# The first two k-tiles of a trunk kernel: scale and shift by TensorE in column groups instead of VectorE dots

## The chip, the cores and the metric

The kernel runs on one core of a Trainium2 chip. The metric is the device time of one execution in microseconds (us), lower is better; a run's time is that of its program on the one core. Before the change the median of three runs is 1251.24 us (1250.53 to 1252.52).

## What is computed

The reference is a two-layer decoder trunk on 256 tokens of width 2048, batch 1. Layer 0 is a Mamba-2 mixer, layer 1 a dilated sliding-window attention over keys and values made from layer 0's output. Only the very beginning of layer 0 matters here:

```python
def _adaln(c, w, b):
    mod = jax.nn.silu(c) @ w + b
    shift, scale, gate = jnp.split(mod, 3, axis=-1)
...
for layer in range(DEPTH):
    shift, scale, gate = _adaln(c, ada_w[layer], ada_b[layer])
    h = x * (1.0 + scale) + shift
    y = _ssd_mixer(h, a_in_w[i], ...)      # proj = h @ in_w; z, xBC, dt = split(proj)
```

`c` is one vector of 2048 numbers, `ada_w` a matrix of 2048 x 6144 for each layer, and `in_w` of layer 0 is 2048 x 10304. So nothing of `h @ in_w` can be computed before a scale and a shift for some of h's 2048 columns have been made out of silu(c) and ada_w.

## The kernel before, in words

**Tiles.** The contraction of 2048 is cut into 16 k-tiles of 128 (kt = 0 to 15). h is kept transposed, 128 rows of a k-tile by 256 tokens, as two tiles: `hhi`, a rounded copy, and `hlo`, what the rounding left (both are named actT in the profile). Weights come as pieces of 512 KB (`raw`, 128 x 1024); each piece is split into `whi` (a copy by ScalarE, L99) and `wlo` (the difference, by VectorE, L101), and TensorE adds three products, hi x hi, hi x lo and lo x hi, into PSUM. There are six buffers of raw and four each of whi and wlo. A piece of the kind "b", "x" or "h" is 24 matmuls of 256 columns (L144 to L146), a piece of the kind "z" 12 of 512 (L198 to L200).

**Scale and shift.** silu(c) stands in all 128 partitions (`cb_`, 1 MB, a broadcast load, L63, and a SiLU by ScalarE, L68). A "column" of ada_w (`araw`, 1 MB, L272) holds, in each partition, the 2048 weights of one output; VectorE multiplies it by cb_ and sums along the row (the dot, L279). Two columns, scale and shift, make a k-tile's modulation; the bias `adab` is added (L284), ScalarE makes h (L444) and its rounded copy (L445), VectorE the remainder (L446). `h_step` does one column; two buffers in each of two pools hold four columns.

**The order of the work.** The begin stage runs through a list of 58 pieces, written out by hand in eight rows, such as "b4:0. b6:0. h z2:0. b2:0 x1:0 h". "z6:2" is piece 2 (k-tiles 4 and 5) of the output block z6; "h" is one of the 16 pieces of the first two blocks, which are accumulated through the whole stage. The list is made so that each piece needs only the k-tiles whose scale and shift exist by then: partial sums of a block are put away in SBUF (`put_away`, L519) and taken up again later. In each step of the loop a piece is fetched (five to six ahead), the next one is split, the piece's matmuls are issued, and about four columns are dotted for seven pieces (`h_step`). All loads of the stage are issued by SyncE's queue, in the order of the program, each waiting for its buffer and for the load eight places before it. After the stage follow the blocks' remaining products, the state-space scan, the output projection and layer 1; none of that is touched.

Of the kernel before, what the change touches and what calls it, by code (L numbers as in the profile page):

```python
# [18 lines left out]
P = 128  # L19
L = 256  # L20
# [29 lines left out]
def trunk(ctx, tc, xT, x, c, par, cst, bias, lnrow, ada, wdt, win, wxs, wout, wk, wv, wbin, wbout, out):  # L50
# [16 lines left out]
    bcast(cb_, c)  # L67
    S.activation(cb_, cb_, AF.Silu)  # L68
# [4 lines left out]

    cons.tile([P, 32], F32, name="pad")
# [243 lines left out]
    with ExitStack() as cA:  # L318
# [14 lines left out]
        with ExitStack() as cS:  # L333
# [4 lines left out]
            begun = {("z", 0): (win[6], 6, szt[0]), ("z", 1): (win[7], 4, szt[1]),  # L338
                     ("xs", 1): (win[5], 4, as_cm(y[0])), ("bc", 2): (win[1], 4, as_cm(y[1])),
                     ("z", 2): (win[8], 14, y[2]), ("bc", 4): (win[2], 12, as_cm(y[3])), ("z", 4): (win[10], 6, y[4]),  # L340
                     ("bc", 6): (win[3], 12, as_cm(y[5])), ("z", 6): (win[12], 10, y[6]), ("z", 5): (win[11], 8, y[7])}
# [39 lines left out]
            def product(kind, g, pre=None):  # L381
# [5 lines left out]
                if src is None:  # L387
                    src = win[{"bc": g // 2, "xs": 4 + g, "z": 6 + g}[kind]]
# [23 lines left out]
            with ExitStack() as c0:  # L412
# [4 lines left out]
                raws, xts, late = [], {}, []  # L417
# [10 lines left out]
                def h_step():  # L428
# [4 lines left out]
                    if kind == "scale" and kt % 2 == 0 and kt:  # L433
                        fetch_x(kt)
                    ada_dot(0, kind, kt, raw)
                    if kt > 1:
                        pin[0] = None
# [11 lines left out]
                h_step.i = 0  # L449
# [5 lines left out]
                for row in ("b4:0. b6:0. h z2:0. b2:0 x1:0 h", "b2:1. x1:1. z1:0 z1:1. z4:0 h h",  # L455
# [3 lines left out]
                    for w in row.split():  # L459
                        if w == two:  # L460
                            n = -2 if sum(o[0] == -2 for o in order) == sum(o[0] == -1 for o in order) else -1
                            order.append((n, sum(o[0] == n for o in order), False))
                        else:
                            order.append((w[:2], int(w[3]), w[-1] == "."))
                order[-5:-5] = [("dt", 0, False), ("dt", 1, False)]
                source = {"dt": wdt, -2: win[0], -1: win[4], **{n: p[0] for n, p in zip(names, begun.values())}}
                pss = {-2: first[0], -1: first[1]}
# [6 lines left out]

                fetch()
                fetch()
                fetch_x(0)
                nc.sync.dma_start(adab_, par[:, :NB])
                V.tensor_scalar(adab[:, :, :, 1:3], adab[:, :, :, 1:3], 1.0, None, op0=ALU.add)
# [3 lines left out]
                fetch_piece()  # L483
                for _ in range(2):
                    for _ in range(2):
                        h_step()
                    while late:
                        pin[0] = late.pop()().ins
                    fetch_piece()
# [31 lines left out]
                begin, done, ended, halves = {}, set(), [], {}  # L521
                for i, (k, q, ends) in enumerate(order):
                    fetch_piece()
                    if i == 16:
                        nc.sync.dma_start(prm, par[:, NB:])
# [10 lines left out]
                    z = str(k)[0] == "z"  # L536
# [4 lines left out]
                    if z:  # L541
# [8 lines left out]
                    while h_step.i < min(len(cols), 4 + (i + 1) * 4 // 7):  # L550
# [118 lines left out]
            def firsts(kind, g):  # L669
# [3 lines left out]
                if src is None:  # L673
                    src = win[{"bc": g // 2, "xs": 4 + g, "z": 6 + g}[kind]]
# [443 lines left out]
def _layout(x, c, ada_w, ada_b, ln_g, ln_b, a_in_w, a_conv_w, a_conv_b, a_dt_bias,  # L1118
# [29 lines left out]
    def mask(delta, win_, dil):  # L1148
# [6 lines left out]
    ada = ada_w.reshape(2, D, 3, KT, P).transpose(0, 2, 3, 4, 1)  # L1155
# [4 lines left out]
    win = _pieces(np.concatenate([bc, xs[:, :1024], z], 1))  # L1160
    return {
        "xT": x[0].T.reshape(KT, P, L).transpose(1, 0, 2), "x": x[0], "c": c, "par": par, "cst": cst, "bias": bias,
# [25 lines left out]
```

## Time and profile before

| what | value |
|---|---|
| median of three runs | 1251.24 us |
| the profiled execution's own time | 1249.66 us |
| its span on the core | 1247.9 us |
| TensorE (PE) busy | 1216.1 us, 97% |
| VectorE (DVE) busy | 1030.6 us, 83% |
| ScalarE (ACT) busy | 703.4 us, 56% |
| moved by DMA | 335.88 MB, 269 GB/s on the mean |
| granted TensorE clock | 0.999 of full |

The profile is of one execution. A row of the timeline has the start in us from the span's start, the duration, the engine, the source line, the operation, the tile written and the tile read, the shapes and a count, and in brackets how long the engine had been idle and what released it. PEld is TensorE's weight load, SPq are the loads as SyncE issues them. A row of stretches has, for each engine, its busy time and in brackets the number of instructions; then the granted clock (PEclk), the mean busy share of the 16 DMA engines, and GB/s. A row of waits has the engine and line that waited, the one it waited for, the sum in us, how often, and the longest.

### The profile page before, as it was taken

How to read it: one execution, taken by the hardware profiler on the slowest of the kernel's cores; microseconds unless marked ns; L12 is line 12 of the kernel's file. 1: busy time of each engine (PE TensorE's matmuls, PEld its weight loads, DVE VectorE, ACT ScalarE, POOL GpSimd, SP SyncE). 2: the span in 40 equal slices, each digit the busy share in tenths (PEclk: the TensorE clock that was granted, in tenths of full speed). 3: DMA queues.
4: the chain of work that ended last, by engine and by line, in shares of the span. 5: the costliest groups of instructions: out<-in, count | busy, mean ns of one | idle time of the engine just before them, and what ended most of it. 6: DMA issues, size and time to landing. Idle time of an engine off the chain costs nothing.

```text
span 1247.9 us, 18743 instructions
## 1 busy us (share of the span) xinstructions
PE 1216.1 (97%) x7086; PEld 1041.6 (83%) x7086; DVE 1030.6 (83%) x1454; ACT 703.4 (56%) x1045; POOL 0.2 (0%) x4
## 2 busy tenths in 40 slices
PE   4999999999999999999999999999999999999997
PEld 4889998898888888778888788888888888888886
DVE  6999986999987989899768678879888867658777
ACT  3655477869588789654344544434445645445631
POOL 0000000000000000000000000000000000000000
PEclk9999999999999999999999999999999999999999
DMA  9999977687556456689988469989998774363641
GB/s 384 423 421 421 421 258 257 223 281 272 203 184 220 164 174 203 224 327 332 360 318 301 179 203 372 372 321 348 357 380 317 240 243 136 135 201 121 235 171 67
DMA packets 80586, 335.88 MB, mean 269 GB/s; under 512 B 9104, under 2 KB 9328, under 8 KB 67696
## 3 DMA queue, kind: packets, MB, share of 16 engines
q1 hardware_dynamic: 80496, 334.69, 73.5%
q8 instruction: 55, 0.90, 0.3%
q14 instruction: 35, 0.29, 0.1%
HBM read 332.47 MB, written 2.18 MB: 268 GB/s over the span
## 4 chain that ended last, share of the span: by engine, by line
PE 85%; DVE 7%; DMA 3%; ACT 2%; issue 2%; SPq 0%; DVEq 0%; ACTq 0%
PE acc L173 21%; PE acc L199 12%; PE acc L200 12%; PE acc L198 12%; PE acc L176 11%; PE acc L144 3%; PE acc L146 3%; PE acc L145 3%; DVE araw L279 2%; DVE wlo L101 2%; PE py L656 1%; DMA araw<-in_ada 1%; ACT whi L99 1%; DMA raw<-in_wv 1%; PE acc L851 1%
## 5 line engine op out<-in xcount | busy, mean ns | idle before, releaser
L99 ACT ACTIVATE whi<-raw 128x1024 fp32r<-128x1024 f32 x392 | 411.7, 1059 | 377.3 <-PE acc L200 144.1
L101 DVE TENSOR_TENSOR wlo<-raw,whi 128x1024 fp32r<-128x1024 f32 x392 | 473.8, 1222 | 137.0 <-ACT whi L99 132.6
L173 PE MATMUL acc<-actT,whi 128*128 128x512 f32 x1280 | 405.3, 397 | 0.0
L176 PEld LDWEIGHTS acc<-actT,wlo 128*128 128x128 f32 x1280 | 239.1, 188 | 59.1 <-DVE wlo L101 4.3
L199 PE MATMUL acc<-wlo,actT 128*128 128x512 f32 x688 | 269.8, 392 | 0.6 <-DVE wlo L101 0.5
L198 PE MATMUL acc<-whi,actT 128*128 128x512 f32 x688 | 266.5, 394 | 1.2 <-ACT actT L723 1.2
L176 PE MATMUL acc<-actT,wlo 128*128 128x256 f32 x1280 | 253.4, 279 | 1.7 <-DVE wlo L101 1.4
L279 DVE SCALAR_TENSOR_TENSOR araw<-araw,cb__72 128x2048 f32<-128x2048 f32 x96 | 219.4, 2286 | 12.0 <-DMA araw<-in_ada 11.9
L173 PEld LDWEIGHTS acc<-actT,whi 128*128 128x128 f32 x1280 | 195.9, 189 | 0.4
L200 PE MATMUL acc<-whi,actT 128*128 128x512 f32 x432 | 169.0, 391 | 0.0
L199 PEld LDWEIGHTS acc<-wlo,actT 128*128 128x128 f32 x688 | 129.3, 188 | 28.8 <-DVE wlo L101 2.8
L198 PEld LDWEIGHTS acc<-whi,actT 128*128 128x128 f32 x688 | 128.8, 188 | 27.0 <-ACT actT L723 1.7
L144 PE MATMUL acc<-actT,whi 128*128 128x256 f32 x384 | 108.9, 287 | 17.4 <-ACT actT L445 17.2
L145 PE MATMUL acc<-actT,whi 128*128 128x256 f32 x384 | 108.7, 285 | 0.0
L146 PE MATMUL acc<-actT,wlo 128*128 128x256 f32 x384 | 106.7, 285 | 1.9 <-DVE wlo L101 1.9
L200 PE MATMUL acc<-whi,ylo 128*128 128x512 f32 x256 | 100.7, 394 | 0.0
L200 PEld LDWEIGHTS acc<-whi,actT 128*128 128x128 f32 x432 | 81.1, 188 | 16.6
L144 PEld LDWEIGHTS acc<-actT,whi 128*128 128x128 f32 x384 | 74.1, 194 | 18.8 <-ACT actT L445 17.4
L146 PEld LDWEIGHTS acc<-actT,wlo 128*128 128x128 f32 x384 | 73.3, 194 | 2.2 <-DVE wlo L101 2.1
L145 PEld LDWEIGHTS acc<-actT,whi 128*128 128x128 f32 x384 | 74.5, 194 | 0.3
L200 PEld LDWEIGHTS acc<-whi,ylo 128*128 128x128 f32 x256 | 48.1, 188 | 9.7
L614 ACT ACTIVATE seg<-cbc,cumT 128x128 f32<-128x128 f32 x128 | 41.0, 390 | 4.9 <-DVE wlo L101 2.3
(262 smaller groups left out, 1054.6 us busy)
## 6 DMA issues: line engine op xcount, KB each, us to landing
araw<-in_ada SPq DMA_DIRECT2D x96, 1024.0 KB, 7.5
raw<-in_win SPq DMA_DIRECT2D x112, 512.0 KB, 6.7
raw<-in_wout SPq DMA_DIRECT2D x64, 512.0 KB, 5.4
raw<-in_wbin SPq DMA_DIRECT2D x64, 512.0 KB, 4.0
raw<-in_wxs SPq DMA_DIRECT2D x48, 512.0 KB, 4.4
raw<-in_wv SPq DMA_DIRECT2D x48, 512.0 KB, 6.3
raw<-in_wk SPq DMA_DIRECT2D x48, 512.0 KB, 7.5
cbc<-cumd SPq DMA_DIRECT2D x16, 512.0 KB, 5.0
```

The source lines that it names most:

```text
L99: copied.append(S.activation(hi, raw, AF.Copy))
L101: latest.append(V.tensor_tensor(lo, raw, hi.bitcast(F32), op=ALU.subtract))
L144: T.matmul(o, hi[:, k, c_], ahi[:, kt, :], start=first, stop=False, skip_group_check=True)
L145: T.matmul(o, hi[:, k, c_], alo[:, kt, :], start=False, stop=False, skip_group_check=True)
L146: T.matmul(o, lo[:, k, c_], ahi[:, kt, :], start=False, stop=kt == k1 - 1, skip_group_check=True)
L173: T.matmul(ps[n], hi[:, k, n * P:n * P + P], both(kt), start=kt == 0, stop=False, skip_group_check=True)
L176: T.matmul(ps[n][:, 0, :], lo[:, k, n * P:n * P + P], high(kt), start=False, stop=kt == KT - 1, skip_group_check=True)
L198: T.matmul(o, h_, hi[:, k, :], start=kt == k0, stop=False, skip_group_check=part)
L199: T.matmul(o, h_, lo[:, k, :], start=False, stop=False, skip_group_check=part)
L200: end = T.matmul(o, l_, hi[:, k, :], start=False, stop=kt == k1 - 1, skip_group_check=part)
L279: V.scalar_tensor_tensor(raw, raw, 1.0, cb_, op0=ALU.mult, op1=ALU.mult, accum_out=mod[layer][:, ct, j:j + 1])
L614: S.activation(seg[:, hh, b, :], cbc[:, hh, b, :], AF.Relu, bias=cumT[:, b, h0 + hh:h0 + hh + 1], scale=-1.0)
```

## The change

- **K-tiles 0 and 1 by TensorE.** Their columns of ada_w are laid out by rows instead (contraction in the partitions): four loads of 512 KB for each k-tile, each 128 x 1024, that hold four groups of 256 outputs (128 of shift, 128 of scale). c comes a second time as a small column tile (128 x 16, `ccol`); ScalarE's SiLU writes it into `ctile`, one column of every 32, the others zero. `ada_partial` runs four matmuls for each load, one for each group of 32 output partitions ("column group"), 256 columns wide, in fp32. `ada_sum` copies the 128 x 256 result (ScalarE), sums over the partitions by two matmuls against a column of ones, adds the bias (VectorE) and makes hhi (ScalarE) and hlo (VectorE, two instructions). The other 28 columns of layer 0's scale and shift stay dots.
- **Filler matmuls.** `keep_warm` runs 128 x 128 matmuls of ones into a PSUM tile that nobody reads: 10 at the start, 12 around k-tile 0's sums.
- **Buffers.** K-tile 0's four loads and k-tile 1's last lie in raw buffers, k-tile 1's first three in wlo buffers.
- **Loads.** The column of c and the bias adab are issued by ScalarE's queue; all others by SyncE's. The broadcast of c comes in two halves, behind the first four pieces, and its SiLU in two halves.
- **The "h" pieces.** The first two blocks (512 columns each, two k-tiles in a piece) become one of 1024 columns with one k-tile in a piece (`whead`, `head_piece`); still 16 pieces of 24 matmuls. The list begins with two of them: "h h b4:0. b6:0. z2:0. b2:0 x1:0", then "h b2:1. x1:1. z1:0 z1:1. z4:0 h"; the other six rows are unchanged.
- **Columns.** One more column is fetched ahead than before.

The order in which SyncE issues its loads at the start, before (names: cb_ is the broadcast of c, araw a column, xt two k-tiles of x, raw a piece):

```order
L63 DMA cb__72<-in_c 128x2048
L272 DMA araw_126<-in_ada 128x2048
L272 DMA araw_128<-in_ada 128x2048
L426 DMA xt_130<-in_xT 128x512
L478 DMA adab_75<-in_par 128x96
L93 DMA raw_134<-in_win 128x1024
L93 DMA raw_136<-in_win 128x1024
L272 DMA araw_138<-in_ada 128x2048
```

and of the changed kernel at the same place:

```order
L423 DMA raw_145<-in_ada 128x1024
L454 DMA xt_149<-in_xT 128x512
L91 DMA raw_151<-in_whead 128x1024
L423 DMA wlo_153<-in_ada 128x1024
L423 DMA wlo_155<-in_ada 128x1024
L423 DMA wlo_157<-in_ada 128x1024
L423 DMA raw_159<-in_ada 128x1024
L91 DMA raw_161<-in_whead 128x1024
L91 DMA raw_163<-in_win 128x1024
L91 DMA raw_165<-in_win 128x1024
L63 DMA cb__72<-in_c 128x1024 x2
L270 DMA araw_169<-in_ada 128x2048
```

Three more loads of k-tile 0 stand ahead of that piece. c has moved from the first place to the one behind k-tile 1's rows and four pieces, and adab is gone from this queue.

The order of SyncE's loads in the middle of the stage, before; raw_843 is piece z6:1, raw_861 is z6:2, raw_886 is z6:3, raw_908 is z6:4:

```order
L272 DMA araw_841<-in_ada 128x2048
L93 DMA raw_843<-in_win 128x1024
L93 DMA raw_861<-in_win 128x1024
L272 DMA araw_880<-in_ada 128x2048
L93 DMA raw_886<-in_win 128x1024
L93 DMA raw_908<-in_win 128x1024
L272 DMA araw_939<-in_ada 128x2048
```

and of the changed kernel, where raw_900 is z6:1, raw_923 is z6:2, raw_941 is z6:3 and raw_966 is z6:4:

```order
L91 DMA raw_900<-in_win 128x1024
L454 DMA xt_918<-in_xT 128x512
L270 DMA araw_921<-in_ada 128x2048
L91 DMA raw_923<-in_win 128x1024
L91 DMA raw_941<-in_win 128x1024
L270 DMA araw_960<-in_ada 128x2048
L91 DMA raw_966<-in_win 128x1024
L91 DMA raw_988<-in_win 128x1024
```

The column that stood between z6:2 and z6:3 now stands between z6:1 and z6:2: of each pair of pieces between two columns, the second has become the first of the next pair.

The diff, cut to its core:

```diff
-    cb_ = cons.tile([P, D], F32, name="cb_")
-    bcast(cb_, c)
-    S.activation(cb_, cb_, AF.Silu)
+    ccol = cons.tile([P, 32], F32, name="pad")[:, :KT]
+    nc.scalar.dma_start(ccol, cT)
...
+                def ada_partial(pp, q, raw):
+                    for j in range(4):
+                        T.matmul(pp[32 * j:32 * j + 32, :], ctile[:, 4 * q + j, :], raw[:, L * j:L * j + L],
+                                 start=q == 0, stop=q == 3, skip_group_check=True)
+                def ada_sum(kt, pp):
+                    part = cs[:, 2 + kt, :]
+                    S.activation(part, pp, AF.Copy)
+                    keep_warm(4 - 4 * kt)
+                    pc = mm.tile([P, 2, L], F32, name="acc")[:, 0, 0:2]
+                    for j in range(2):
+                        T.matmul(pc[:, j:j + 1], part[:, j * P:j * P + P], ones[:, 0:1], start=True, stop=True)
+                    keep_warm(8 - 8 * kt)
+                    V.tensor_tensor(mod[0][:, kt, 0:2], pc, adab[:, 0, kt, 0:2], op=ALU.add)
+                    x_, t = xts[0][:, kt, :], pe.tile([P, L], F32, name="htmp")
+                    S.activation(hhi[:, kt, :], x_, AF.Identity, bias=shift(0, kt), scale=scale(0, kt))
+                    V.tensor_scalar(t, x_, scale(0, kt), shift(0, kt), op0=ALU.mult, op1=ALU.add)
+                    return V.tensor_tensor(hlo[:, kt, :], t, hhi[:, kt, :].bitcast(F32), op=ALU.subtract)
...
-                for row in ("b4:0. b6:0. h z2:0. b2:0 x1:0 h", "b2:1. x1:1. z1:0 z1:1. z4:0 h h",
+                for row in ("h h b4:0. b6:0. z2:0. b2:0 x1:0", "h b2:1. x1:1. z1:0 z1:1. z4:0 h",
...
+                keep_warm(10)
+                rows0 = [ada_rows(0, q) for q in range(4)]
+                nc.scalar.dma_start(adab_, par[:, :NB])
+                fetch_x(0)
+                fetch_piece()
+                rows1 = [ada_rows(1, q, wp.tile([P, 1024], F32R, name="wlo", bufs=4).bitcast(F32) if q < 3 else None)
+                         for q in range(4)]
...
+                for q in range(4):
+                    ada_partial(pp[1], q, rows1[q])
+                    head_piece(0, halves[0], (2 * q, 2 * q + 1))
...
-                    while h_step.i < min(len(cols), 4 + (i + 1) * 4 // 7):
+                    while h_step.i < min(len(cols), 4 + (i + (i > 7)) * 4 // 7):
```

105 lines of the change are left out of this document (71 added, 34 removed).

## The prediction

> **What bounds the kernel now.** I read the page first, for the span, then the busy times in stretches of the first 190 us, since the diff touches only the stage that ends there.
>
> ```profile
> span 1247.9 us, 18743 instructions
> core 0: us, PE busy (x) PEld busy (x) DVE busy (x) ACT busy (x) POOL busy (x), PEclk, DMA share, GB/s
> 0.00:2.00 2.00, 0.00 (x0) 0.00 (x0) 0.17 (x2) 1.27 (x1) 0.20 (x4) 1.00 0.30 57
> 2.00:15.00 13.00, 0.03 (x1) 0.03 (x1) 5.22 (x7) 3.85 (x6) 0.00 (x0) 1.00 0.97 384
> 15.00:40.00 25.00, 20.70 (x136) 19.11 (x137) 22.83 (x26) 12.05 (x18) 0.00 (x0) 1.00 1.02 423
> 40.00:80.00 40.00, 40.00 (x250) 36.21 (x249) 37.04 (x39) 24.57 (x34) 0.00 (x0) 1.00 1.02 421
> 80.00:120.00 40.00, 40.00 (x239) 35.74 (x238) 36.92 (x40) 21.35 (x28) 0.00 (x0) 1.00 1.02 422
> 120.00:155.00 35.00, 35.00 (x283) 34.51 (x282) 34.13 (x36) 16.91 (x20) 0.00 (x0) 1.00 1.02 421
> 155.00:190.00 35.00, 34.63 (x221) 31.01 (x219) 29.78 (x53) 25.93 (x37) 0.00 (x0) 1.00 0.68 242
> ```
>
> The reader is to see two things at once. TensorE (PE) is empty for 15 us and then has 20.70 of 25 us, so about 19.3 us are lost before 40 us, and none from there to 155 us. And the DMA engines are full (share 1.02, 421 to 423 GB/s in every stretch) from 15 to 155 us, with DVE at 92 to 98%. Only after 155 us does the traffic fall. So the stage has two lines that run side by side: TensorE's work and the stream of loads. The waits say how far apart they are, first those up to 40 us, then (last row) the longest from 40 to 165 us.
>
> ```profile
> PE acc L144 <- ACT actT L445: 17.2, 2, 15.0
> DVE araw L279 <- DMA araw<-in_ada: 7.7, 2, 7.1
> PE acc L146 <- DVE wlo L101: 1.9, 1, 1.9
> ...
> ACT whi L99 <- DMA raw<-in_win: 38.1, 25, 3.4
> ```
>
> TensorE's lost time is the 15.0 us until the first k-tile of h is there, a second wait of 2.2 and one of 1.9. After 40 us ScalarE waits 25 times for a weight piece to land: the pieces are split as they land, and TensorE takes each a little later. So an earlier TensorE catches up with the stream, and the question is how much room there is.
>
> **The start, part by part.** Its rows:
>
> ```profile
> 0.73 0.39 SPq L63 DMA_DIRECT2D cb__72<-in_c  x1
> 5.46 1.91 ACT L68 ACTIVATE cb__72<-cb__72 128x2048 f32<-128x2048 f32 x1 [3.45 <-DMA cb__72<-in_c]
> 8.06 2.29 DVE L279 SCALAR_TENSOR_TENSOR araw<-araw,cb__72 128x2048 f32<-128x2048 f32 x1 [7.06 <-DMA araw<-in_ada]
> 10.43 2.29 DVE L279 SCALAR_TENSOR_TENSOR araw<-araw,cb__72 128x2048 f32<-128x2048 f32 x1
> 13.07 0.60 ACT L444 ACTIVATE htmp<-xt,mod 128x256 f32<-128x256 f32 x1 [5.70 <-DVE mod L284]
> 14.52 0.40 ACT L445 ACTIVATE actT<-htmp 128x256 fp32r<-128x256 f32 x1
> 14.97 0.79 PE L144 MATMUL acc<-actT,whi 128*128 128x256 f32 x2 [14.97 <-ACT actT L445]
> 42.48 0.28 PE L144 MATMUL acc<-actT,whi 128*128 128x256 f32 x1
> ```
>
> Three loads of 1 MB (c, then scale and shift of k-tile 0) land at 5.4, 8.0 and 10.4, about 2.5 us each; two dots of 2.29 us and a chain of small steps follow. The change puts the 2 MB of k-tile 0 first, as four loads: they land at about 4.2, 5.4, 6.7 and 7.95. Each is used by four matmuls of 256 columns in full fp32, whose price the trace has elsewhere:
>
> ```profile
> 218.69 0.60 PE L601 MATMUL aux<-bcm 128*128 128x256 f32 x2
> 219.13 0.38 PE L602 MATMUL aux<-bcm 128*128 128x128 f32 x2
> 229.60 0.45 PE L656 MATMUL py<-xd,seg 128*64 128x64 f32 x8
> ```
>
> A matmul of 256 columns is two records and 0.44 us from start to start (218.69 to 219.13). Whether four column groups run beside each other no row shows; for two groups of 64 the last row does: 8 records of 64 columns take 0.45 us in all, hardly more than the 0.38 of two of 128. So I take 0.44 us a load (low end 0.44, high end 4 x 0.44 = 1.8). The last load is then summed at 7.95 + 0.44 + 0.25 for the end of the pipe = 8.6; the copy (0.42, as L445), two one-column matmuls (0.4, a guess between nothing and 0.6), the bias on DVE (0.16) and h on ScalarE (0.60) give 10.3; two half copies of the first piece (0.55 each, the first counts) let TensorE start at about 10.9 instead of 14.97. ScalarE's table load of 1.28 us and SiLU wait for the small column of c; even at 5.5 us they are hidden by the second load. The 10 + 12 filler matmuls (0.22 each at the full pace, twice that cold) fill waits; cover gone, they cost up to 4 us, of the start alone.
>
> K-tile 1's four loads stand behind x and the first piece, so they land by 15.1; the same chain makes h at 17.4, and the second piece, copied after it in 1.05 us, starts on TensorE at about 18.5. From there 24-matmul pieces follow at 2.9 us: six of the first seven are done by 33.5 and all seven by about 36.7. Before, seven pieces were done at 42.48 (the last row of the start). So the **lead is 5.8 us** there, about 2 us of it because those matmuls no longer run cold:
>
> ```profile
> 18.99 0.41 PE L144 MATMUL acc<-actT,whi 128*128 128x256 f32 x1
> 19.21 0.41 PE L145 MATMUL acc<-actT,whi 128*128 128x256 f32 x1
> ...
> 24.82 0.28 PE L145 MATMUL acc<-actT,whi 128*128 128x256 f32 x1
> 24.94 0.28 PE L146 MATMUL acc<-actT,wlo 128*128 128x256 f32 x1
> ```
>
> (0.21 us from start to start before 19.6, 0.12 after.) c now lands behind four pieces and the rows of k-tile 1, at about 21; its SiLU lies on ScalarE before the dot of k-tile 2 needs it, at about 24, so that costs nothing while ScalarE has its 25 us half empty.
>
> **What of the lead is late next.** The stream carries the same loads in the same amount: 16 pieces of in_whead take the place of as many, ada's 2 MB for k-tiles 0 and 1 are cut differently, c is still 1 MB. What changes is the order, and the second pair of lists above shows it: each column (1 MB, 2.5 us) now stands one piece earlier, so every second piece has 1 MB more ahead of it. The tightest is z6:2. Its neighbour z6:3 has the same bytes ahead of it in both kernels (within 0.05 MB); the rows of before are z6:2's wlo, z6:3's copy, and z6:2's first matmul:
>
> ```profile
> 100.80 1.23 DVE L101 TENSOR_TENSOR wlo<-raw,whi 128x1024 fp32r<-128x1024 f32 x1 [0.52 <-ACT whi L99]
> 102.37 1.06 ACT L99 ACTIVATE whi<-raw 128x1024 fp32r<-128x1024 f32 x1 [1.60 <-DMA raw<-in_win]
> 103.69 0.39 PE L198 MATMUL acc<-whi,actT 128*128 128x512 f32 x1
> ```
>
> z6:3 landed at 102.3. In the changed order z6:2 lands one piece (0.52 MB at 422 GB/s = 1.24 us) ahead of that, at 101.1; its copy ends at 102.15, its wlo at 103.3 (the dot of the column before it, 2.29 us from 99.8, is over by then). TensorE needs wlo two matmuls of 0.23 after its start, so it can start at 102.85 at the earliest, **0.85 us** before its start of now. The same sum for the other pieces leaves more room. After 155 us TensorE is the bound again and keeps what it has. So of 5.8 us some 5 go back as small waits for pieces, between 40 and 105 us.
>
> Added to the 0.85 is whatever the whole stream gains. One line of the DMA view of the first 80 us, in slices of 2 us, shows what is to be had:
>
> ```profile
> GB/s 57 336 422 406 403 285 426 436 412 446 408 444 406 446 399 414 432 412 424 434 406 436 414 440 408 408 442 404 438 410 428 422 432 418 416 435 411 398 436 410
> ```
>
> The slice from 10 to 12 us, in which x and the 384-byte rows of adab are moved, has 285: 0.65 us lost. adab now comes on ScalarE's queue, at the start, and a column of c in 64-byte rows is added there. If they cost the stream nothing, 0.65 is gained; if both cost as adab did, as much is lost. [...] No run here shows a load on ScalarE's queue.
>
> **Sum.** 0.85 + 0.1 = 0.95 us. The profiled execution took 1249.66 us (span 1247.9 and 1.8 around it), so the changed one would take 1248.7; the median of the three runs is 1.6 above that execution, so I predict **1250.3 us**. By the bounds of the stream (0.2 to 1.5 us) it is 1249.7 to 1251.0. A measurement of this kernel can tell about 0.2%, 2.5 us, from no change, so this is "the same".
>
> **The rivals.**
> (a) The stream isn't the limit: 421 GB/s is what TensorE's pace asks for, since SyncE's queue waits for free buffers, and it rises when TensorE is earlier. Then the lead of 5.8 us stays: 1245.4. For it: TensorE doesn't wait once after 40 us. Against: the share of 1.02 and the same 421 to 423 in four stretches of differing work, and the 25 waits of ScalarE for landings. [...]
> (b) The column groups don't run beside each other. Then a k-tile costs 16 x 0.44 = 7.0 us of TensorE instead of 1.8. K-tile 0 is done at about 17.0 and k-tile 1 at about 29, 11 later than above; seven pieces end near 47 instead of 42.5 and the kernel is about 4.5 us slower: 1255.7. It decides from a start that is 4.9 us later than mine; anything less is swallowed by the lead that is thrown away anyway. Against: L656.
> (c) VectorE becomes the bound. Per seven pieces it has four dots of 2.29, seven splits of about 1.15 and 1.1 of small steps, 18.3 us, where the stream takes 19.3 (8.1 MB). Its queue now has the dot of a newly landed column ahead of the splits; if each group of seven loses over 1 us to waits for landings, TensorE falls behind by the rest; 0.6 us more in each of six groups is 3.6 us, less the 0.95: 1253.9. For it: DVE is at 92 to 98%. Against: dot and copy end at the same moment, 102.1.
> (d) The start isn't earlier (TensorE cold between k-tiles, ScalarE late): same time within the forecast's own range, by the 4.9 us above.
>
> **Chances.** Forecast with (d) 0.76, (a) 0.12, (b) 0.05, (c) 0.07. Faster by over 0.2% only by (a): 0.12; slower by (b) and (c): 0.12; the same 0.76. The range takes in the forecast's own and reaches half way to (a), whose lead may stay in part, and to (c): 1247.5 to 1253.0.
>
> **What would show it.** TensorE's first weight matmul near 11 and the second piece near 18.5; the first seven pieces done near 37; then TensorE's waits for wlo or whi, some 5 us in all, between 37 and 105, where there are none now; DMA still at 421; z6:2 starting near 102.8 and everything behind 155 us about 1 us earlier. Wrong, if the stretches from 40 to 120 us show TensorE without a gap (a), matmuls of L429 at 0.44 apart (b), or DVE at 100% with DMA below 415 (c).

## The result, and the profile after

| | before | changed |
|---|---|---|
| median (runs) | 1251.18 us (16) | 1253.48 us (16) |
| ratio to before, 95% interval | | 1.0021 (1.0014 to 1.0027) |
| the same once more (a0) | 1251.41 us (21) | 1253.96 us (11), 1.0018 (1.0009 to 1.0027) |
| profiled execution: time, span | 1249.66, 1247.9 us | 1251.80, 1250.0 us |

The change costs 2.3 to 2.6 us. The forecast was 1250.3 us, 0.95 us less than before, with a range up to 1253.0: wrong in sign, and 1253.5 lies just above that range. First the stretches of the changed kernel, to be laid beside the prediction's:

```profile
span 1250.0 us, 18993 instructions
core 0: us, PE busy (x) PEld busy (x) DVE busy (x) ACT busy (x) POOL busy (x), PEclk, DMA share, GB/s
2.00:15.00 13.00, 10.13 (x80) 7.67 (x79) 1.19 (x4) 3.30 (x6) 0.00 (x0) 1.00 1.00 367
15.00:40.00 25.00, 22.66 (x173) 19.81 (x173) 15.22 (x17) 14.13 (x20) 0.00 (x0) 0.93 1.02 423
40.00:80.00 40.00, 38.95 (x235) 34.51 (x234) 39.33 (x43) 22.60 (x31) 0.00 (x0) 1.00 1.02 421
80.00:120.00 40.00, 40.00 (x239) 35.75 (x238) 38.10 (x39) 20.94 (x29) 0.00 (x0) 1.00 1.02 423
120.00:155.00 35.00, 35.00 (x289) 34.78 (x288) 33.71 (x38) 16.49 (x21) 0.00 (x0) 1.00 1.02 421
```

Look at DVE, not at PE. VectorE has 1.19 and 15.22 us of work in the first two rows where it had 5.22 and 22.83; then it is full (39.33 of 40), and in that row TensorE, which had 40.00 of 40 before, has 38.95. The 10.13 us of PE before 15 us are fillers and row products; its first weight matmul comes at 14.77, hardly earlier than before's 14.97. The start and the second piece (L429: row products, L509: fillers, L544: weight matmuls):

```profile
5.07 1.28 ACT L419 ACT_TABLE_LOAD   x1 [5.07 <-DMA pad<-in_cT]
6.64 0.64 PE L429 MATMUL acc<-raw,xs 128*32 128x256 f32 x8 [0.96 <-ACT xs L419]
10.30 1.38 PE L509 MATMUL acc<-ones 128*128 128x128 f32 x10
11.62 0.64 PE L429 MATMUL acc<-raw,xs 128*32 128x256 f32 x8
14.77 0.39 PE L544 MATMUL acc<-actT,whi 128*128 128x256 f32 x1 [1.41 <-ACT whi L535]
20.18 0.64 PE L429 MATMUL acc<-raw,xs 128*32 128x256 f32 x8
23.76 0.58 PE L544 MATMUL acc<-actT,whi 128*128 128x256 f32 x1 [1.83 <-ACT whi L97]
```

And VectorE behind it (L277: a column's dot, L99: a piece's low half):

```profile
27.53 2.29 DVE L277 SCALAR_TENSOR_TENSOR araw<-araw,cb__72 128x2048 f32<-128x2048 f32 x1 [0.30 <-ACT cb__72 L554]
40.37 2.29 DVE L277 SCALAR_TENSOR_TENSOR araw<-araw,cb__72 128x2048 f32<-128x2048 f32 x1
42.58 2.29 DVE L277 SCALAR_TENSOR_TENSOR araw<-araw,cb__72 128x2048 f32<-128x2048 f32 x1
45.02 1.23 DVE L99 TENSOR_TENSOR wlo<-raw,whi 128x1024 fp32r<-128x1024 f32 x1
46.53 2.28 DVE L277 SCALAR_TENSOR_TENSOR araw<-araw,cb__72 128x2048 f32<-128x2048 f32 x1
48.74 2.36 DVE L99 TENSOR_TENSOR wlo<-raw,whi 128x1024 fp32r<-128x1024 f32 x2
```

c lands at 24.88, the first dot starts at 27.53, and from 40 us on the dots of k-tiles 3 and 4 stand in VectorE's queue in front of the low halves that TensorE takes next: the half of b2:1 is begun at 45.02, that of x1:1 at 48.74. In the kernel before, two low halves (L101) stand between one dot and the next at this place; here there are none and one:

```profile
37.39 2.29 DVE L279 SCALAR_TENSOR_TENSOR araw<-araw,cb__72 128x2048 f32<-128x2048 f32 x1 [0.61 <-DMA araw<-in_ada]
39.83 1.23 DVE L101 TENSOR_TENSOR wlo<-raw,whi 128x1024 fp32r<-128x1024 f32 x1
41.95 1.23 DVE L101 TENSOR_TENSOR wlo<-raw,whi 128x1024 fp32r<-128x1024 f32 x1 [0.52 <-ACT whi L99]
43.10 2.28 DVE L279 SCALAR_TENSOR_TENSOR araw<-araw,cb__72 128x2048 f32<-128x2048 f32 x1
```

The waits of TensorE from 24 to 110 us in the changed kernel show what came of it:

```profile
PE acc L544 <- ACT whi L97: 1.8, 1, 1.8
PE acc L144 <- DVE wlo L99: 1.0, 2, 0.6
```

To see what a wait is worth at the end, I count TensorE's matmuls from the last one back and compare the start of each with the same matmul of the kernel before. Two of the places are telling: the start of the ninth piece of the list, which in the changed kernel is b2:1 ("at b2:1"; 45.37 us in before, where the ninth piece is x1:1), and the place at 67.65 us. "Half clock" is the number of stretches, before 40 us, in which the clock records show half the clock. A stretch is 3.41 us long; one of e8's, two of e6's and all of e7's are twice that. The records begin at 4 to 21 us, so what lies ahead of them isn't counted.

| run | ratio (95%) | at b2:1 | at 67.65 | at 140 us | half clock |
|---|---|---|---|---|---|
| changed | 1.0021 (1.0014 to 1.0027) | -0.17 | +1.56 | +1.56 | 1 |
| changed, again (a0) | 1.0018 (1.0009 to 1.0027) | +1.76 | +3.50 | +3.50 | 2 |
| before, again (b0) | one run | +0.45 | +0.45 | +0.45 | 1 |
| e1 no fillers | 1.0011 (1.0002 to 1.0019) | -0.89 | +0.86 | +1.11 | 2 |
| e2 small loads on SyncE's queue | 1.0010 (1.0001 to 1.0018) | +1.18 | +2.92 | +2.92 | 2 |
| e8 both of these | 1.0023 (1.0014 to 1.0032) | +0.79 | +2.53 | +2.53 | 2 |
| e9 more fillers | 1.0019 (1.0010 to 1.0028) | +3.29 | +5.03 | +5.03 | 1 |
| e3 columns first | 1.0026 (1.0017 to 1.0035) | +3.97 | +4.81 | +4.81 | 3 |
| e4 a column later | 1.0041 (1.0029 to 1.0053) | +3.04 | +3.37 | +3.37 | 2 |
| e5 splits first | 1.0037 (1.0024 to 1.0050) | +3.61 | +6.85 | +6.85 | 3 |
| l1 no sums, splits first | 1.0025 (1.0014 to 1.0036) | -3.22 | +3.26 | +3.26 | 2 |
| l3 one load less | 1.0030 (1.0018 to 1.0042) | +1.55 | +3.14 | +3.14 | 2 |
| l4 = l1 and l3 | 1.0010 (0.9999 to 1.0020) | -2.69 | +1.02 | +1.02 | 1 |
| l5 no dots of k-tiles 2, 3 | 1.0007 (0.9998 to 1.0015) | +1.55 | +1.55 | +1.55 | 2 |
| l6 no sums, no dots | 1.0007 (0.9998 to 1.0015) | -2.56 | +0.07 | +1.06 | 1 |
| l7 = l6 and one load less | 1.0000 (0.9988 to 1.0012) | -3.05 | -2.07 | -1.21 | 2 |
| b2 before, columns in halves | 1.0003 (0.9993 to 1.0013) | +2.25 | +2.25 | +2.25 | 1 |
| e6 only k-tile 0 by TensorE | 1.0066 (1.0053 to 1.0079) | +8.37 | +8.37 | +8.37 | 3 |
| e7 the same, no fillers | 1.0064 (1.0051 to 1.0077) | +7.60 | +7.61 | +7.60 | 3 |

(us; + is later than before; one profiled execution each, so the ratio, from all runs, is the verdict. Behind 182 us a single profile gains or loses up to 2.5 us more, e4 4.7, in a part of the kernel whose code the change leaves as it was.)

### The profile page after: what moved, and what is told of

It is laid out like the page before. It is cut to its first block, busy times and chain, and to the rows that moved or that the text cites. A ratio compares the mean times of both kernels' runs of the same rounds, so it can differ in the third digit from the quotient of the medians.

```text
span 1250.0 us, 18993 instructions
## 1 busy us (share of the span) xinstructions
PE 1231.0 (98%) x7202; PEld 1052.1 (84%) x7202; DVE 1023.1 (82%) x1449; ACT 702.4 (56%) x1048; POOL 0.2 (0%) x4
## 4 chain that ended last, share of the span: by engine, by line
PE 85%; DVE 6%; DMA 5%; ACT 2%; issue 2%; SPq 0%; DVEq 0%; ACTq 0%
PE acc L171 21%; PE acc L197 13%; PE acc L198 12%; PE acc L196 12%; PE acc L174 10%; PE acc L142 2%; PE acc L144 2%; PE acc L143 2%; DVE wlo L99 2%; DMA raw<-in_wk 1%; PE py L726 1%; DVE araw L277 1%; PE acc L547 1%; PE acc L546 1%; PE acc L544 1%
## 5 line engine op out<-in xcount | busy, mean ns | idle before, releaser
L99 DVE TENSOR_TENSOR wlo<-raw,whi 128x1024 fp32r<-128x1024 f32 x391 | 471.7, 1220 | 132.1 <-ACT whi L97 124.6
L174 PEld LDWEIGHTS acc<-actT,wlo 128*128 128x128 f32 x1280 | 239.0, 188 | 59.8 <-DVE wlo L99 5.1
L174 PE MATMUL acc<-actT,wlo 128*128 128x256 f32 x1280 | 253.5, 279 | 2.0 <-DVE wlo L99 1.3
L277 DVE SCALAR_TENSOR_TENSOR araw<-araw,cb__72 128x2048 f32<-128x2048 f32 x92 | 210.1, 2284 | 4.2 <-DMA araw<-in_ada 2.9
L171 PEld LDWEIGHTS acc<-actT,whi 128*128 128x128 f32 x1280 | 195.9, 189 | 0.4
L144 PE MATMUL acc<-actT,wlo 128*128 128x256 f32 x256 | 71.5, 284 | 1.0 <-DVE wlo L99 1.0
L142 PE MATMUL acc<-actT,whi 128*128 128x256 f32 x256 | 72.2, 284 | 0.0
L143 PE MATMUL acc<-actT,whi 128*128 128x256 f32 x256 | 72.0, 283 | 0.0
L144 PEld LDWEIGHTS acc<-actT,wlo 128*128 128x128 f32 x256 | 48.6, 192 | 1.5 <-DVE wlo L99 1.5
L142 PEld LDWEIGHTS acc<-actT,whi 128*128 128x128 f32 x256 | 49.0, 192 | 0.4
L143 PEld LDWEIGHTS acc<-actT,whi 128*128 128x128 f32 x256 | 49.1, 192 | 0.1
```

Source lines behind the costliest of these rows:

```text
L99: latest.append(V.tensor_tensor(lo, raw, hi.bitcast(F32), op=ALU.subtract))
L142: T.matmul(o, hi[:, k, c_], ahi[:, kt, :], start=first, stop=False, skip_group_check=True)
L143: T.matmul(o, hi[:, k, c_], alo[:, kt, :], start=False, stop=False, skip_group_check=True)
L144: T.matmul(o, lo[:, k, c_], ahi[:, kt, :], start=False, stop=kt == k1 - 1, skip_group_check=True)
L171: T.matmul(ps[n], hi[:, k, n * P:n * P + P], both(kt), start=kt == 0, stop=False, skip_group_check=True)
L174: T.matmul(ps[n][:, 0, :], lo[:, k, n * P:n * P + P], high(kt), start=False, stop=kt == KT - 1, skip_group_check=True)
```

## The experiments

**Theories.** Three were left after the two traces: the loads' stream (all landings are later than worked out), the late columns (VectorE starts late and writes low halves behind dots), TensorE's start. The half clock came up on the way.

**e1, e2: TensorE's start, and the small loads.**

```diff
-                    keep_warm(4 - 4 * kt)
...
-                    keep_warm(8 - 8 * kt)
```

> The twelve filler matmuls round k-tile 0's sums go (0.28 us each in the profile of the changed kernel, some 3.3 us of the 14.77 us that pass before TensorE's first weight matmul). If the late start decides the time, the first weight matmul comes at about 11.5 us and the end about 3 us earlier: 1250.5. If the loads' stream decides (z6:2's piece lands at 102.97 us instead of before's 102.5 or so), or VectorE's dots before b2:1, the start moves by 2 to 3 us and the end by at most 0.4: 1253.1 to 1253.5.

```diff
-    nc.scalar.dma_start(ccol, cT)
+    nc.sync.dma_start(ccol, cT)
...
-                nc.scalar.dma_start(adab_, par[:, :NB])
+                nc.sync.dma_start(adab_, par[:, :NB])
```

> c's column and ada's bias go back from ScalarE's queue to SP's, the column as its first load, the bias behind k-tile 0's rows. Theory of the stream (two queues of small packets beside the first large loads lose about 2 us that a saturated stream never gives back): the landings come 1 to 2 us earlier all the way to z6:2, and so does the end, 1251.5 to 1252.5. Theory of the late columns (VectorE has no dot before 27.5 us, then is behind at b2:1 and x1:1): the same loads in nearly the same order, the time stays at 1253.2 to 1253.7. If the start decides: the column lands at about 3 us instead of 4.99, the first weight matmul 2 us earlier, and the end with it.

e1's first weight matmul came at 12.46 us, 2.3 earlier, yet TensorE still lost 1.75 us at b2:1 and x1:1 and ended at 1.0011. In e2 the column of c landed at 2.32 us instead of 4.99, the first weight matmul came at 14.37, and the landings were no earlier. Both intervals overlap the changed kernel's, so the two went together with another run, e8:

> The changed kernel without the twelve fillers, and with c's column and ada's bias on SP's queue again. Each alone came to 1.0011 and 1.0010 of before instead of 1.0021. If they work on different limits (TensorE's start; the queue): 1.0000 to 1.0003. If they only touch one limit, or are chance: 1.0008 to 1.0015. By the floor that the stream sets, no lower than 1.0004 to 1.0007.

1.0023: nothing adds up, and the gains of e1 and e2 are not shown to be any. The queue on which the small loads are issued isn't the stream's trouble: issuing them on the other one brought no weight piece earlier, z6:2's rows land at 103.85 us in e2 and at 102.97 in the changed kernel.

**e3, e4: columns earlier, columns later.** In e3 c's halves and k-tile 2's first column are issued ahead of pieces b4:0 and b6:0; e4 has one `fetch()` fewer in the second step of the loop.

```diff
                 fetch_piece()
-                fetch_piece()
-                fetch_piece()
...
                 fetch()
                 fetch_x(2)
+                fetch_piece()
+                fetch_piece()
```

> c's two halves and the first columns of k-tile 2 are issued ahead of the pieces b4:0 and b6:0 (two pieces, 2.5 us of the stream). Theory of the late columns: the first dot comes at about 25 us instead of 27.53, the splits of b2:1 and x1:1 no longer wait behind two dots, TensorE loses about 2 us less at these pieces and the whole run is 1.5 to 2 us shorter: 1251.5 to 1252. Theory of the stream: the gaps at b2:1 and x1:1 close, but z6:2 still waits for its landing at 103 us, and the time stays within 0.5 us: 1253.0 to 1253.5.

```diff
                     if i == 1:
                         fetch()
-                        fetch()
```

> One column fewer runs ahead, so that from the middle of the stage each column stands where it stood before, one piece later than in the changed kernel. By the prediction's own reasoning (the end follows z6:2's landing) z6:2's rows land one column, 1.24 us, earlier: 1252.2 to 1252.5, if VectorE is not what is late there. If the columns come too late as it is, their dots come later still, and the time goes to 1253.5 to 1254.5.

Neither gained; e3's interval overlaps the changed kernel's, e4's lies above it. e3 had c 3.6 us earlier (21.26) but its first dot at 29.08, since SiLU of c stands in ScalarE's queue behind k-tile 1's sums, and those came late. Its dots of k-tile 3 did come 0.9 us earlier with respect to b2:1 (the first of them ends 3.44 us ahead of it instead of 2.55), and TensorE lost 0.84 us between the two places instead of 1.73. In e4 the dots of k-tile 3's second column and of k-tiles 4 and 5 ended 7.7 to 9.5 us later than in the kernel before; in the changed kernel it is 2.1 to 5.2 us. Yet its profile loses only 0.33 us between the two places, and 4.7 us behind 182 us, where a half-clock stretch of 6.83 us falls, at 232 us. So columns later didn't pay, and columns earlier, at the cost of pieces, didn't either, but e4 doesn't say by what way.

**e5, l1: the splits first; and the sums left out.** In e5 three dots wait for the low half of the next piece. l1 has that, and leaves out the row products and their sums:

```diff
+                    if 7 <= h_step.i - 1 <= 9:
+                        pin[0] = latest[-1].ins
                     ada_dot(0, kind, kt, raw)
```

> VectorE's eighth to tenth dot (k-tile 3's second column, k-tile 4's two) are held back until the low half of the next piece is written; in the changed kernel two dots stood ahead of b2:1's split (45.02 us) and one ahead of x1:1's (48.74 us), and TensorE lost 1.6 us there. If TensorE's own lateness decides the end, the two gaps close and the end comes 1.6 us earlier: 1251.9 as a median. If the loads' stream decides (z6:2's rows land at 102.97 us, and its first matmul can start 1.75 us behind that, at 104.7 instead of 105.25), it gains at most 0.5: 1253.0. If VectorE decides through its sum of work, the dots only move and the time stays at 1253.5.

> As the kernel with the splits first, and besides k-tiles 0 and 1 take their scale and shift from the bias alone: the row products, their sums and the waits on the rows are left out, the loads stay. TensorE can then start when the first weight piece has landed and is split, about 13 us instead of 14.8, go into the second piece without the 3 us of waiting at 20.8 us, and save 2.4 us of row products. If the start decides, that is a lead of 5 us or more over the changed kernel at the eighth piece, and the end comes up to 5 us earlier: 1248.5. If the loads' stream decides, z6:2 still lands at about 103 us and the time is that of the kernel with the splits first, within 0.5: 1252.5 to 1253.

A miss for every theory: e5 came to 1.0037. l1 shows why, in ScalarE's waits from 15 to 60 us and TensorE's from 24 to 110:

```profile
ACT htmp L469 <- DVE mod L282: 4.5, 2, 3.7
```

```profile
PE acc L142 <- ACT whi L97: 2.8, 1, 2.8
```

A dot that is held back makes its k-tile's h late, and h (L469) stands in ScalarE's queue ahead of the copies of the next pieces; so TensorE waits for `whi` instead of `wlo`. In l1 a lead of 3.22 us at b2:1 was 3.26 us of lag at 67.65 us; up to 1.7 us of that (an estimate, half its length) is a half-clock stretch of 3.41 us that began at 48.56 us, behind the wait of 2.8 us. So this early start, with its dots held back, bought nothing.

**l3, l4: the stream.** Both leave out one load of 1 MB (k-tile 4's first column; the dot reads c twice); l4 has l1's edits as well.

```diff
+                    if i == 8:
+                        raws.append(wp1.tile([P, D], F32, name="araw", bufs=2))
-                    if i < len(cols):
+                    elif i < len(cols):
```

> The changed kernel without the load of k-tile 4's first column (1 MB, 2.48 us of the stream); its dot reads c twice instead and takes as long. All loads behind it, z6:2's among them, land 2.5 us earlier; TensorE and VectorE have the same work. If the loads' stream decides: 1251.0, the end 2.5 us earlier. If TensorE is itself late (start, and the splits behind the dots), it waits for nothing there and the time stays within 0.4: 1253.1 to 1253.9.

> The splits first, no row products or sums for k-tiles 0 and 1, and k-tile 4's first column not loaded: both limits moved. If TensorE's lateness and the stream are two limits that stand within 0.5 us of one another, only this run gains what each seems to offer: 2.5 us or more against the changed kernel, 1251 or less, and more than the two single ones together. If the start alone decides it equals the run without the sums.

A shorter stream alone buys nothing (1.0030); l4, at 1.0010, is below l1's 1.0025, with intervals that overlap.

**l5, l6, l7: VectorE's dots, then all three.** In l5 the dots of k-tiles 2 and 3 are not made.

```diff
-                    ada_dot(0, kind, kt, raw)
+                    if kt > 3:
+                        ada_dot(0, kind, kt, raw)
```

> The changed kernel with the four dots of k-tiles 2 and 3 left out (these k-tiles take their values from the bias alone); the columns are still loaded. VectorE has 9.2 us less to do between 27 and 45 us, and the backlog in which it wrote b2:1's and x1:1's low halves late does not arise. If VectorE's late start is what the changed kernel pays for, TensorE's two gaps go (1.6 us) and more where the backlog had delayed it: 1251.9 or less. If the loads' stream or TensorE's start decides, the time stays at 1253 to 1253.5, as in the run with one load less and in the run without the sums.

> No row products and sums for k-tiles 0 and 1, and no dots for k-tiles 2 and 3: TensorE is some 2.7 us ahead of the kernel before at 46 us, as in the run without the sums, and VectorE has nothing to catch up, so that the lead is not lost at the next pieces. If VectorE was what ate it: 1249 or less, and far below both single runs. If the stream decides, z6:2 lands at 103 us as ever, and the time is 1252 to 1253.

This is the edit that does it. l5's stretches, and then those of the repeated changed kernel (a0), which has the same two half-clock stretches:

```profile
15.00:40.00 25.00, 22.66 (x159) 19.24 (x160) 10.16 (x12) 15.07 (x22) 0.00 (x0) 0.86 1.02 422
40.00:80.00 40.00, 40.00 (x251) 36.22 (x249) 35.96 (x37) 21.84 (x30) 0.00 (x0) 1.00 1.02 421
```

```profile
15.00:40.00 25.00, 22.62 (x157) 18.71 (x158) 14.20 (x16) 12.95 (x19) 0.00 (x0) 0.86 1.02 423
40.00:80.00 40.00, 38.94 (x235) 34.50 (x235) 38.85 (x40) 22.52 (x31) 0.00 (x0) 1.00 1.02 421
```

To 40 us TensorE is the same (22.66 and 22.62); behind it l5 has not one gap, a0 1.06 us of them. In the table the six profiles that have the changed kernel's order of columns and dots (changed, a0, e1, e2, e8, e9) all lose 1.73 to 1.75 us between b2:1 and 67.65, whatever they brought there, from 0.89 ahead to 3.29 behind; l3, without one column's load, loses 1.59, and l5 0.00. By the medians l5 stands 0.0011 to 0.0014 lower, 1.4 to 1.7 us, though its interval just touches the changed kernel's. The clock is not what sets them apart: at the same granted clock of 0.997, seven executions of l5 took 1251.3 us on the mean and eleven of the changed kernel 1253.6. And l6, with a lead of 2.56 us on top, has the very same 1.0007: something else takes that lead. In l6 and, without its load, in l7, z6:2's rows (the copy starts as they land):

```profile
102.70 1.06 ACT L97 ACTIVATE whi<-raw 128x1024 fp32r<-128x1024 f32 x1 [1.63 <-DMA raw<-in_win]
...
104.28 0.61 PE L196 MATMUL acc<-whi,actT 128*128 128x512 f32 x2
```

```profile
100.43 1.06 ACT L97 ACTIVATE whi<-raw 128x1024 fp32r<-128x1024 f32 x1 [1.69 <-DMA raw<-in_win]
```

> No row products and sums for k-tiles 0 and 1, no dots for k-tiles 2 and 3, and k-tile 4's first column not loaded (its dot reads c twice). The run without sums and dots ended at 1.0007 of before, with TensorE 2 us ahead at 46 us and 1.06 us behind at 140 us. If the loads' stream is the floor there, taking 2.48 us off it lets that lead through: 1.06 us behind becomes 1 us ahead or more, 0.9985 to 0.9992 of before. If something else is the floor (VectorE's remaining work): the same 1.0007, within 0.0004.

The load less brought z6:2's landing from 102.7 to 100.4 and TensorE from 1.06 us late to 1.21 us early at 140 us. So below VectorE the stream is the floor, by these two profiles. It isn't z6:2 alone: of the 3.62 us that l6 loses from b2:1 on, 2.63 are gone by 67.65 us, where l7 loses 0.98. l7's time, 1.0000, goes the same way as far as its interval can tell; it is not the 0.9985 to 0.9992 expected.

**e6, e7: half of the change.** Only k-tile 0 by TensorE; c right behind its rows, k-tile 1 by dots. (k-tile 1's columns are read here from data that is laid out in rows, so its values aren't the reference's.) e7 has no fillers.

```diff
-                raws, xts, late = [None] * 4, {}, []
+                raws, xts, late = [None] * 2, {}, []
...
+                for h in (slice(0, D // 2), slice(D // 2, D)):
+                    bcast(cb_[:, h], c, h.start)
                 fetch_piece()
+                fetch()
+                fetch()
```

> Only k-tile 0 by TensorE's column groups; k-tile 1 by VectorE's dots as before, with c's two halves issued right behind k-tile 0's rows and k-tile 1's columns behind the first weight piece. c lands near 11.5 us instead of 24.88, VectorE's first dot comes near 16 to 17 us instead of 27.53, and TensorE has no row products inside its first piece. If VectorE's late start is the cause, the columns of k-tiles 2 to 4 are done at before's times (30.6, 39.7 and 50.6 us) and the time is at or below before's: 1249.5 to 1251. If TensorE's sums for the second k-tile are worth what they were made for, this loses: 1254 or more.

> The same without the twelve fillers round k-tile 0's sums (3.3 us of its chain): the first weight matmul near 12.5 us. If the start is still late after VectorE has its columns, 1 to 2 us less than with the fillers; if VectorE or the stream then decides, the same time within 0.5.

Here I was furthest off: 1.0066 and 1.0064. The first dot came at 18.55 as planned, but the column loads of k-tiles 2 and 3 had moved ahead of piece z2:0, which landed at 35.07, and TensorE was out of pieces (TensorE's waits from 20 to 60 us in e6):

```profile
PE acc L197 <- DVE wlo L99: 2.4, 1, 2.4
PE acc L543 <- ACT actT L475: 2.0, 1, 2.0
PE acc L196 <- ACT s L582: 1.9, 1, 1.9
```

e7's first weight matmul was 2.4 us earlier than e6's (14.48 and 16.91) with the same time: so there the start isn't the limit. Between b2:1 and 67.65 us neither loses anything, with VectorE's dots early, but TensorE is 8 us late there. With e3 this says that the first 40 us of the stream carry too little for both customers: what is moved ahead for VectorE is taken from TensorE.

**b0, b2: the stream's place.** By its place I mean a landing's time less the bytes landed so far at 421.5 GB/s.

> The kernel before, profiled once more. If its stream always starts as in the first profile, z6:2's rows land near 101 us and TensorE is within 0.5 us of the first profile at 182 us. If the stream's place is chance, its landings differ by 1 to 2 us, as those of the changed kernel's variants do among one another (z6:2's rows between 102.6 and 104).

```diff
+            for h in (slice(0, D // 2), slice(D // 2, D)):
+                nc.sync.dma_start(raw[:, h], ada[layer, KIND.index(kind), ct][:, h])
```

> The kernel before with the columns of k-tiles 0 and 1 loaded in two halves of 512 KB (rows of 4 KB), eight issues for four; all else as before. If the halves' packets are what makes the changed kernel's stream late, landings from 12 us on are 0.5 to 2 us later than in the kernel before and the time rises by up to 1 us (1.0004 to 1.001). If not: landings within 0.3 us, the same time.

Near 100 us the place is 4.5 in before's first profile, 5.2 in b0, 4.8 in b2 and 6.4 in the changed kernel (6.2 in a0; 5.6 to 7.3 in its variants). So 0.7 us of the distance between my two profiles can be chance, and 1.2 or so is left for the change. (z6:2's rows landed at 98.54 us in before's first profile and at 99.34 in b0; the 102.5 that e1's expectation gives for before, and the 101 of b0's, are not its landings.) Loads in halves are not its cause. e6, with k-tile 0's rows alone, has 5.0 (e7 5.2); so most of it comes with k-tile 1's rows, or with what stands around them. In the trace's records a 16 KB packet of instructions, which took 0.96 us, comes at 19.0 us in the changed kernel, where the first after 15 us comes at 35.35 in the kernel before; which of the two costs how much was not separated.

**a0, e9: the clock.** e9 puts fillers round k-tile 1's sums too.

```diff
-                    keep_warm(4 - 4 * kt)
+                    keep_warm(4)
...
-                    keep_warm(8 - 8 * kt)
+                    keep_warm(8 + 8 * kt)
```

> The changed kernel once more: 1.0014 to 1.0027 of before if its first interval holds. Its profile shows whether the one half-clock window after 6 us (23.3 us) and the stream's place (z6:2's rows at 102.97 us) are typical; by its variants one more window and a landing between 102 and 104 are to be expected, and TensorE 1.5 to 3 us behind before at 140 us.

> The changed kernel with fillers round k-tile 1's sums as well (4 ahead, 16 behind; TensorE waits 3 us there at 20.4 to 23.8 us). If that wait is what sends the clock to half behind it (23.3 to 26.8 us, and 10 us apart from others), there is one window less in the first 30 us and TensorE is 1 to 1.7 us earlier at 46 us: 1.0005 to 1.0012 of before. If the windows come whatever TensorE does there, the same as the changed kernel within 0.0005, or up to 0.5 us slower by the fillers.

a0 confirms the result, and its profile is the likelier picture: my first profile of the changed kernel was the fastest of its 16 runs. e9 changed nothing (1.0019), but it doesn't test what it was made for: of the fillers that it adds, all but one stand in TensorE's queue ahead of k-tile 1's sums, and of the wait of 1.83 us before the second piece 1.50 us was left, with a half-clock stretch at 27.41 us right behind it:

```profile
25.09 0.47 PE L509 MATMUL acc<-ones 128*128 128x128 f32 x2
27.06 0.39 PE L544 MATMUL acc<-actT,whi 128*128 128x256 f32 x1 [1.50 <-ACT whi L97]
```

Its first two row products ran at the slow pace too (1.08 us instead of 0.64, at 7 and 9 us). Within e9 the clock counts: the four of its 11 executions with a granted clock of 0.998 or more took 1252.2 us on the mean, the other seven 1254.9. a0 and the first profile differ by 1.93 us at b2:1 and by one half-clock stretch; in the first profile's, from 23.34 to 26.75 us, a matmul of 256 columns starts every 0.21 us, behind it every 0.12. How much of the spread between executions (1251.80 to 1256.45 us) comes of it isn't shown: the changed kernel's 14 executions at 0.996 and 11 at 0.997 both took 1253.6 us on the mean. Nor is it shown whether the changed kernel is at half clock for longer than the kernel before: its executions list 0.995 to 0.999, before's 0.997 to 1.000, but before's records begin only at 19 to 20 us. The 1.74 us don't come of it: they are lost behind 45 us, where none of the six profiles has such a stretch up to 67.65 us.

## Why the prediction was wrong, by its own steps

1. **Column groups side by side:** right. Four matmuls of 256 columns are 8 records in 0.64 us, near the low end of 0.44 to 1.8; rival (b) falls.
2. **Start at 10.9, second piece at 18.5, seven pieces done 5.8 us earlier:** wrong, 14.77, 23.76 and 0.17 (in a0 the seven are done 1.77 us later than before). The sum itself was loose: 2.9 us a piece from 18.5 gives 35.9 for the seven, not 36.7. "Hidden by the second load" failed: c's column landed at 4.99, table load and SiLU followed until 6.6. And the fillers fill no waits: they stand in TensorE's queue between the products, so that the last load, landed at 8.7, was multiplied at 11.62. K-tile 1's last product (20.18) stood behind the first piece's matmuls, 2.9 us after its landing.
3. **"Of 5.8 us some 5 go back":** the mechanism was right where there was a lead: l6's 2.56 us are gone by 140 us, and l7, with 1 MB less to load, keeps 1.21 of its 3.05. (l1 and l4 lose theirs too, but with dots held back.) In the changed kernel there was no lead to give back, and lateness isn't given back: a0, e2, e8 and e9 carry their 0.8 to 3.3 us at b2:1 on to 140 us, and the 1.74 on top. By the prediction's own sum a start up to 4.9 us later was free; the seven pieces were done 5.6 us later than forecast in the first profile and 7.6 in a0. So step 2 alone takes away the 0.95 us that were to be gained. How much it costs beyond that is within chance: b0, the kernel before once more, is 0.45 us late there itself.
4. **c late "costs nothing":** this is the step that failed and made the kernel slower. I put its landing at 21 and the first dot at 24, beside an idle ScalarE, and read "each column stands one piece earlier" off the middle of the list. At its head the columns of k-tiles 2 and 3 land at 27.3, 32.8, 38.0 and 40.5 us, where they had landed at 23.0, 26.8, 29.2 and 37.4; VectorE has 15.22 us of work to 40 us where it had 22.83, and pays back at b2:1 and x1:1. Measured: 1.74 us in six profiles, 1.4 to 1.7 by l5. The landings are not the whole of it. From 15 to 60 us VectorE waits for no column in any of the six profiles; it waits 0.3 us for the SiLU of c, which stands in ScalarE's queue behind k-tile 1's sums and three copies, while c has landed. In a0 c landed at 24.22 us and the first column at 26.66:

```profile
27.04 1.99 ACT L554 ACTIVATE cb__72<-cb__72 128x1024 f32<-128x1024 f32 x2
29.06 2.29 DVE L277 SCALAR_TENSOR_TENSOR araw<-araw,cb__72 128x2048 f32<-128x2048 f32 x1 [0.29 <-ACT cb__72 L554]
```

   So VectorE's dots hang on TensorE's sums and move with TensorE: k-tile 3's first dot ends 2.53 to 2.55 us ahead of the start of b2:1 in all six, which fits that they all lose the same. It starts 2.3 us (changed) to 6.5 us (e9) after its column landed. The last line of the diff has a hand in this: it makes each of the first four dots one step of the loop later (steps 2, 4, 6 and 7, counted from 0, instead of 1, 3, 5 and 6), so that with the fifth dot in step 8 three stand in a row. No run moved the dots alone, so what the order costs without the landings is open.
5. **The stream, +0.1 (bounds -0.65 to +0.65):** mis-sized. No run shows the +0.1; what the runs showed is the stream's place near 100 us, 6.4 us in the changed kernel against 4.5 before, and z6:2's rows no earlier with the small loads back on SyncE's queue (103.85 us in e2, 102.97 in the changed kernel). z6:2's rows were worked out for 101.1 us and its first matmul for 102.85 at the earliest; in the changed kernel:

```profile
103.06 1.06 ACT L97 ACTIVATE whi<-raw 128x1024 fp32r<-128x1024 f32 x1 [1.62 <-DMA raw<-in_win]
...
105.25 0.62 PE L196 MATMUL acc<-whi,actT 128*128 128x512 f32 x2
```

   The copy starts 2 us after the forecast landing (z6:3, with the same bytes ahead of it in both kernels, landed at 102.28 before and lands at 104.28). So even without VectorE's lateness TensorE would be no earlier than in l6, 1.06 us late at 140 us instead of 0.85 early. In the changed kernel itself this floor isn't reached: TensorE is 1.56 us late at 67.65 us already and waits for nothing from 51 to 150 us.
6. **The sum:** in the first profile TensorE is 0.17 us early at b2:1, loses 1.73 at VectorE's dots, and is 1.56 late at 140 us instead of 0.85 early. By the medians l5 takes away 1.4 to 1.7 of the 2.3 to 2.6 us. The 0.9 us (0.0007) that it leaves can't be told from nothing (0.9998 to 1.0015), and its parts are not separated: l5 is held by its own start, 1.55 us late from b2:1 on, and l6, 4.1 us ahead of l5 there, by the stream. What the six profiles lose besides behind 182 us (0.3 to 2.0 us; b0 0.3) no run explains.

Of the rivals, (c), VectorE as the bound, was right in the engine and, by luck, at 1253.9 in the price; its mechanism, a little loss in each group of seven pieces, was not, nor its sign, DMA below 415. (d), no earlier start, happened, but "the same time" did not follow from it: the start came later than the 4.9 us that it had for cover, and VectorE's loss stood on top. What stays open: why the stream is late, what the order of the dots costs by itself, and what decides in an execution how many half-clock stretches fall into its start.

## What to carry to other kernels

When a change takes work off an engine at the start, ask what that engine will do then and whether its next inputs have arrived: here VectorE lost four dots and became later, for its operand c had been moved behind 6.6 MB of other loads, and the SiLU of c behind TensorE's sums. In this stage, whose DMA share is 1.00 from 2 to 15 us and 1.02 from there to 155 us, an earlier consumer earned nothing (l6's lead of 2.56 us was gone by 140 us), a later one stayed late (a0 was 1.76 us late at b2:1 and 3.50 at 140 us), and loads moved ahead moved others back (in e6 piece z2:0 landed at 35.07 us). And delaying work on one engine to let another pass must be followed through the queue of the third: in l1, with dots held back, h waited 4.5 us on ScalarE, and TensorE 2.8 us for the copies that stood behind h.

## What the runs showed of the hardware

TensorE's half clock came in stretches of 3.41 us or twice that (6.83), and in e3 and a0, which had several of them in the first 40 us, they began 10.24 us apart (7.39, 17.63 and 27.87 in e3; 16.15 and 26.39 in a0), three times 3.41. Their place differs between executions of one kernel: the first profile of the changed kernel has its one stretch at 23.34 us. Whether filling the idle time removes them the traces don't show, for e9's fillers left 1.50 us of the wait. Nor did TensorE stand idle all through the 3.41 us ahead of that stretch at 23.34 us: it has 1.49 us of work there.
